# Gated MLP of a two-layer decoder trunk: eight of 44 gate tiles as seven block products instead of eight

## Chip, cores and metric

The kernel runs on one core of one Trainium2 chip. The metric is device time in microseconds (us) of one launch; smaller is better. The engines of that core work from separate queues, each strictly in the order in which the program names the instructions: TensorE (PE in the profile), VectorE (DVE), ScalarE (ACT), GpSimd (POOL) and SyncE (SP), whose queue issues nearly all of the DMAs here.

## What is computed

A decoder trunk of two layers over 256 tokens of width 2048. Each layer has an attention mixer (block-sparse attention in layer 0, latent attention in layer 1) and then a gated MLP with an inner width of 5632. Only the MLP's gate product `h @ w_gate` changes here.

```python
def conv_glu_ffn(h, w_gate, w_up, conv_w, conv_b, w_down):
    g = h @ w_gate
    g = causal_depthwise_conv(g, conv_w, width=3) + conv_b     # along the tokens
    return (jax.nn.silu(g) * (h @ w_up)) @ w_down

for i in range(2):
    x = x + mixer_i(rms_norm(x, attn_norm[i]))
    x = x + conv_glu_ffn(rms_norm(x, ffn_norm[i]), ...)
```

All of it is float32.

## The kernel before

**Three products for one.** Every float32 operand of a large product is split into a high and a low part: the high part is a cast to the type float32r, the low part is the operand minus the high part. A product then takes three matmuls: high by high, high by low, low by high. The normed input `h` of the MLP lies in SBUF as such parts, with features on the partitions: 16 tiles of 128 features, each with 256 high and 256 low token columns. The norm's gain is in `h`; its factor per token (`rstd_b`, spread over the partitions) is multiplied in after the gate and the up product.

**Pieces.** Weights stream from HBM in units of 128 x 1024 words, each of two pieces of 128 x 512. A piece of the MLP's gate or up weight holds four 128 x 128 blocks: four feature tiles of the input (`kq` counts these fours, 0 to 3) by one tile of 128 inner features. `Stream.split` (lines 113 to 130) makes the two parts of a piece: ACT casts (`whi`, line 125), DVE subtracts (`wlo`, line 126). There are five buffers for each part, so that the parts of piece p take the place of those of p - 5.

**The order of the work** is written out by hand. `quanta` lists the steps, one piece each. At step q the main loop (the end of `trunk`) first splits all pieces up to q + 3, then issues the matmuls of piece q, and then whatever `at(q, ...)` has put beside it:

```python
ws.split(q + min(1 + q // 6, AHEAD_PIECES))     # AHEAD_PIECES = 4: pieces below q + 4
f(*args, *ws.take(q))
for g, gargs in (..., *side.pop(q, [])):
    g(*gargs)
```

**The MLP.** `plan_gate_up` goes through 44 tiles of 128 inner features. For each it adds four gate pieces and four up pieces. A piece is 12 matmuls (`feat_major`, lines 301 to 303): for each of its four blocks high weight by high `h`, high weight by low `h`, low weight by high `h`. The weight block is the stationary operand, and the 256 tokens move. Beside the matmuls, by step after a tile's last gate piece q:

- q: `evac_gate` (DVE, line 970), PSUM times `rstd_b` into `g`
- q + 1: `conv_last` (ACT, line 977); q + 2: `conv_rest` (two DVE instructions, line 983); q + 3: `silu` (ACT, line 988)
- q + 4, which is the last up piece: `scaled` and `product` (DVE, lines 991 and 994); then `high` (ACT, line 997) and `low` (DVE, line 1001) make the parts of the inner activation `a`, one of 44 tiles in SBUF.

The down product (`plan_down_feat`) reads `a` after all 44 tiles are there. At the start of a gate and up stage, q0, lie remains of the norm: PE sums at step q0 + 2 (line 370), PE transposes at q0 + 3 (line 380), and then ACT's copy of `rstd_b` (line 384), for which the first `evac_gate` waits. The attention stages have helpers that the change uses too: `cross_out` and `cross_in` turn a matrix by 32 x 32 transposes on DVE (line 410) and a way through HBM (four DMAs out, one back).

Of the kernel before, what the change touches and what calls it, by code (L numbers as in the profile page):

```python
# [54 lines left out]
H_TILES = 0, 4, 16  # L55


class Halves:


    def __init__(self, tiles):
        self.tiles = tiles
# [4 lines left out]
        return self.tiles[i][p, k - H_TILES[i], s]  # L67


class Stream:  # L70

    def __init__(self, nc, raw_pool, part_pool, units, starts):
# [3 lines left out]
        self.pieces = [(u, i, n) for u, (_, k, n) in enumerate(units) for i in range(k)]  # L78
        self.raw, self.parts = {}, {}
        self.loaded = self.split_to = 0  # L80

    def load(self, upto):
# [30 lines left out]
    def split(self, upto):  # L113
        while self.split_to < min(upto, len(self.pieces)):
            i = self.split_to
            u, j, n = self.pieces[i]
            self.load(u + AHEAD_UNITS)
            w = self.raw[u][:, j * n : (j + 1) * n]
            b, c = self.starts(u, j)
            hi = self.part_pool.tile([P, 512 + ROOM], F32R, name="whi")[:, b : b + max(n, 512)]  # L120
            lo = self.part_pool.tile([P, 512 + ROOM], F32R, name="wlo")[:, c : c + max(n, 512)]
            if i == 0:
                self.nc.vector.tensor_copy(hi[:, :n], w)
            else:
                self.nc.scalar.copy(hi[:, :n], w)  # L125
            self.nc.vector.tensor_tensor(  # L126
                lo[:, :n], w, hi[:, :n].bitcast(F32), op=ALU.subtract
            )
# [8 lines left out]
def trunk(ctx: ExitStack, tc: tile.TileContext, a, out):  # L137
# [30 lines left out]
    units += units_of("ffn_gu0")  # L168
    units += units_of("ffn_down0")
    units += units_of("mla_wq_a")  # L170
    units += units_of("mla_wqr")
    units += units_of("mla_wkv_a", 2 * KVN)
# [2 lines left out]
        for name in names:  # L175
            units += grouped(name, 1, g)
    units += units_of("mla_wo")
    units += units_of("ffn_gu1")
    units += units_of("ffn_down1")
    def starts(u, j):  # L180

        if units[u][2] > 512:
            return 0, 0
        return BY_TOKEN if u < 96 or 400 <= u < 444 else BY_FEATURE

    assert len(units) == 740
    ws = Stream(nc, raw_pool, part_pool, units, starts)


    att = ExitStack()  # L190
# [71 lines left out]
    def add(f, *args):  # L262
        quanta.append((f, args))
        return len(quanta) - 1
# [679 lines left out]

    ffn = {}

    def open_ffn(layer):
        if layer == 0:
            att.close()
        else:  # L950
            att2.close()
        ffn["stack"] = ExitStack()
        ffn["pool"] = ffn["stack"].enter_context(tc.tile_pool(name=f"ffn{layer}", bufs=2))
        ffn["a"] = ffn["pool"].tile([P, NF, 2 * S], F32R, name="a", bufs=1)
        ffn["g"] = [ffn["pool"].tile([P, S + 2], F32, name=f"g{i}", bufs=1) for i in range(2)]
        for g in ffn["g"]:
            nc.vector.memset(g[:, 0:2], 0.0)

    class FTile:
        def __init__(self, layer, j, norm):  # L960
            self.layer, self.j, self.norm = layer, j, norm
            self.gate, self.up = {}, {}

        def cw(self, i):
            c = C_CW + (self.layer * 3 + i) * NF + self.j
            return par[:, c : c + 1]

        def evac_gate(self):
            self.g = ffn["g"][self.j % 2]
            nc.vector.tensor_tensor(  # L970
                self.g[:, 2:], self.gate["acc"][:, :S], self.norm.rstd_b, op=ALU.mult
            )
# [26 lines left out]
        def low(self):  # L999
# [2 lines left out]
                a_[:, self.j, S:], self.c, a_[:, self.j, :S].bitcast(F32), op=ALU.subtract  # L1002
            )

    def plan_gate_up(layer, norm):
        for j in range(NF):
            f = FTile(layer, j, norm)
            for kind, st in (("g", f.gate), ("u", f.up)):
                for kq in range(4):
                    q = add(lambda t_hi, t_lo, n, st=st, kq=kq: feat_major(  # L1010
                        st, lambda: norm.h, 4 * kq, KD - 1, kq == 0, t_hi, t_lo, n))
                if kind == "g":
                    if j == 0:
                        at(q, open_ffn, layer)
                    at(q, f.evac_gate)
                    at(q + 1, f.conv_last)
                    at(q + 2, f.conv_rest)
                    at(q + 3, f.silu)
                    at(q + 4, f.scaled)
                else:  # L1020
                    at(q, f.product)
                    at(q + 1, f.high)
                    at(q + 2, f.low)

    plan_gate_up(0, n2)

# [362 lines left out]
    ffn["stack"].close()  # L1389


def wo_order(opened):
# [106 lines left out]
```

## Time and profile before

| | |
|---|---|
| median of three runs | 2069.29 us (2069.16 to 2069.46) |
| span of the profiled execution, first to last instruction | 2067.4 us; what lies outside it is 1.9 us by the median (the page has no other time for that execution) |
| busy: PE, DVE, ACT | 2060.5, 1424.4, 1157.9 us |
| matmuls | 16588 |
| granted TensorE clock | 1.000 |
| moved by DMA | 410.92 MB, mean 199 GB/s |
| first and last gate evacuation | 382.3 us in layer 0, 1819.3 us in layer 1 |

Busy is the time in which an engine had at least one instruction in flight. Matmuls overlap, so the pace of PE is read from the distance of their starts, not from the duration of one. In rows of a timeline the first number is the start, the second the duration; in square brackets stands how long the engine had been idle before and what it waited for.

### The profile page before, as it was taken

What the parts mean: (1) busy time and instruction counts of PE and PEld (TensorE: products, weight loads), DVE (VectorE), ACT (ScalarE), POOL (GpSimd) and SP (SyncE); (2) the same over time, 40 slices, a digit from 0 to 9 for tenths busy, and PEclk for the clock granted to TensorE, in tenths of its full rate; (3) what the DMA queues carried; (4) which work ended last, traced back from release to release, by engine and by line L of the source; (5) the groups of instructions that cost most, each with busy time, mean ns of one, the idle gap of its engine ahead of it and who ended that gap; (6) DMA issues with size and microseconds to landing.
All of it is one profiled execution on the core that took longest, in us unless ns stands there. A gap on an engine that the chain in (4) does not pass through costs nothing.

```text
span 2067.4 us, 42691 instructions
## 1 busy us (share of the span) xinstructions
PE 2060.5 (100%) x16588; PEld 1994.8 (96%) x16588; DVE 1424.4 (69%) x2780; ACT 1157.9 (56%) x2238; POOL 51.1 (2%) x38
## 2 busy tenths in 40 slices
PE   9999999999999999999999999999999999999999
PEld 7888899999999999999999889999999999999999
DVE  7877777766676667655556998767666766665554
ACT  6656666555555555555555786655555555554443
POOL 0000000000000000000000110000000000000000
PEclk9999999999999999999999999999999999999999
DMA  7777776555555565555555646555555565566663
GB/s 276 232 245 224 232 235 209 192 193 195 194 194 194 194 194 195 197 194 193 196 194 158 215 145 189 195 190 191 195 196 195 192 194 195 195 201 202 196 210 125
DMA packets 128251, 410.92 MB, mean 199 GB/s; under 512 B 15008, under 2 KB 28832, under 8 KB 128048
## 3 DMA queue, kind: packets, MB, share of 16 engines
q1 hardware_dynamic: 127728, 407.84, 60.3%
q8 instruction: 129, 2.11, 0.4%
q14 instruction: 74, 0.61, 0.1%
q10 hardware_dynamic: 288, 0.33, 0.1%
q0 software_dynamic: 32, 0.04, 0.0%
HBM read 396.48 MB, written 11.67 MB: 197 GB/s over the span
## 4 chain that ended last, share of the span: by engine, by line
PE 96%; DVE 2%; DMA 1%; ACT 0%; issue 0%; POOL 0%; SPq 0%; DVEq 0%; ACTq 0%; POOLq 0%
PE acc L301 26%; PE acc L303 26%; PE acc L302 26%; PE acc L275 14%; DVE wlo L126 1%; PE sc L551 0%; PE sc L549 0%; PE sc L550 0%; DMA raw<-in_mla_wqn 0%; PE sc L652 0%; PE sc L571 0%; PE tp L542 0%; DVE ss L454 0%; DMA xT<-in_xT 0%; ACT sq L450 0%
## 5 line engine op out<-in xcount | busy, mean ns | idle before, releaser
L126 DVE TENSOR_TENSOR wlo<-raw,whi 128x512 fp32r<-128x512 f32 x1464 | 998.7, 689 | 370.6 <-ACT whi L125 366.5
L125 ACT CAST whi<-raw 128x512 fp32r<-128x512 f32 x1463 | 870.1, 618 | 458.6 <-PE acc L302 215.3
L301 PE MATMUL acc<-h,whi 128*128 128x256 f32 x2880 | 796.1, 276 | 0.0
L303 PE MATMUL acc<-h,wlo 128*128 128x256 f32 x2880 | 795.8, 276 | 0.0
L302 PE MATMUL acc<-h,whi 128*128 128x256 f32 x2880 | 795.7, 276 | 0.0
L301 PEld LDWEIGHTS acc<-h,whi 128*128 128x128 f32 x2880 | 540.8, 188 | 0.0
L302 PEld LDWEIGHTS acc<-h,whi 128*128 128x128 f32 x2880 | 540.8, 188 | 0.0
L303 PEld LDWEIGHTS acc<-h,wlo 128*128 128x128 f32 x2880 | 540.8, 188 | 0.0
L302 PE MATMUL acc<-a,whi 128*128 128x256 f32 x1408 | 389.0, 276 | 0.0
L301 PE MATMUL acc<-a,whi 128*128 128x256 f32 x1408 | 389.0, 276 | 0.0
L303 PE MATMUL acc<-a,wlo 128*128 128x256 f32 x1408 | 389.0, 276 | 0.0
L275 PE MATMUL acc<-whi,h 128*128 128x512 f32 (+1 forms) x896 | 266.1, 378 | 0.7 <-ACT h L323 0.7
L301 PEld LDWEIGHTS acc<-a,whi 128*128 128x128 f32 x1408 | 264.4, 188 | 0.0
L302 PEld LDWEIGHTS acc<-a,whi 128*128 128x128 f32 x1408 | 264.4, 188 | 0.0
L303 PEld LDWEIGHTS acc<-a,wlo 128*128 128x128 f32 x1408 | 264.4, 188 | 0.0
L275 PEld LDWEIGHTS acc<-whi,h 128*128 128x128 f32 x896 | 164.9, 188 | 31.1 <-ACT h L323 1.2
L275 PE MATMUL acc<-wlo,h 128*128 128x512 f32 (+1 forms) x448 | 168.7, 377 | 0.2 <-DVE wlo L126 0.2
L301 PE MATMUL acc<-oT,whi 128*128 128x256 f32 x512 | 142.7, 279 | 0.0
L303 PE MATMUL acc<-oT,wlo 128*128 128x256 f32 x512 | 141.7, 277 | 0.0
L302 PE MATMUL acc<-oT,whi 128*128 128x256 f32 x512 | 141.6, 277 | 0.0
L970 DVE TENSOR_TENSOR g<-acc,rstd_b 128x256 f32<-128x256 f32 x88 | 37.5, 426 | 126.8 <-PE acc L303 123.9
L977 ACT ACTIVATE c<-g,par 128x256 f32<-128x256 f32 x88 | 53.1, 603 | 107.8 <-DVE g L970 107.8
(197 smaller groups left out, 1616.2 us busy)
## 6 DMA issues: line engine op xcount, KB each, us to landing
raw<-in_ffn_gu SPq DMA_DIRECT2D x352, 512.0 KB, 4.4
raw<-in_ffn_down SPq DMA_DIRECT2D x176, 512.0 KB, 4.7
raw<-in_moba_wk SPq DMA_DIRECT2D x32, 512.0 KB, 5.7
raw<-in_moba_wv SPq DMA_DIRECT2D x32, 512.0 KB, 5.3
raw<-in_moba_wo SPq DMA_DIRECT2D x32, 512.0 KB, 4.5
raw<-in_mla_wo SPq DMA_DIRECT2D x32, 512.0 KB, 4.0
raw<-in_moba_wq SPq DMA_DIRECT2D x24, 512.0 KB, 6.2
there<-blk SPq DMA_DIRECT2D x36, 128.0 KB, 2.5
```

Of the source, the lines that this page charges most:

```text
L125: self.nc.scalar.copy(hi[:, :n], w)
L126: self.nc.vector.tensor_tensor(lo[:, :n], w, hi[:, :n].bitcast(F32), op=ALU.subtract)
L275: mm(state["acc"][t][:, :n], src[:, kt, c : c + P], (t_lo if part == 1 else t_hi)[:, :n], start=kt == 0 and part == 0, stop=kt == k_last a ...
L301: mm(o, w_hi, src[:, kt, :S], start=first and k == 0, stop=False, skip_group_check=True)
L302: mm(o, w_hi, src[:, kt, S:], start=False, stop=False, skip_group_check=True)
L303: mm(o, w_lo, src[:, kt, :S], start=False, stop=kt == k_last, skip_group_check=True)
L970: nc.vector.tensor_tensor(self.g[:, 2:], self.gate["acc"][:, :S], self.norm.rstd_b, op=ALU.mult)
L977: nc.scalar.activation(self.c, self.g[:, 2:], AF.Identity, bias=par[:, cb : cb + 1], scale=self.cw(2))
```

## The change

In each layer eight of the 44 gate tiles, in two groups of four (tiles 15 to 18 and 19 to 22), are no longer four pieces each. The product of a group is taken for each `kq` as a two by two block product, tokens (two halves of 128) by inner features (two pairs of tiles) by features (even and odd tiles), in the scheme that needs seven products of sums of blocks in place of eight products of blocks (15 additions). For each of the four `kq` of a group there are seven block pieces of six matmuls, so 168 matmuls for a group where four tiles took 192. Here a token block is the stationary operand, and 256 weight columns move. The sums over the four `kq` lie in four PSUM banks for the length of a group.

Four sums of token blocks are made at the start of each stage, in four rounds three steps apart (`tokens`: four ACT instructions; `token_sums`: two DVE instructions in each of two steps; `token_high`: ACT; `token_low`: DVE). The weights of a group's gate tiles come by loads of their own, four of 256 KB for each `kq`; four sums of weight blocks for each `kq` are DVE instructions. After a group the seven sums are mixed (`mixed`, five DVE instructions in three steps) and turned to features on the partitions (`cross`: two DVE transposes and four DMAs, `crossed`: one DMA). `evac_gate` of a block tile reads that in place of PSUM, just ahead of the tile's up pieces.

The order: 24 plain pieces; 28 times one block piece and two plain ones; four plain pieces; again 28 times; then what is left. Plain pieces keep their form; the tile of `a` is cut in four, and the parts that are filled last hold the raw weights, the token sums and the mixed sums until then.

The diff, cut (the class `Inner`, the unit lists and the offsets of the layer-1 weights are left out; by the latter some pieces of the latent attention and of its output product lie at other offsets in their buffers):

```diff
+BLOCK_LEAD, BLOCK_GAP, BLOCK_EVERY = 24, 4, 2
+BLOCK_GROUPS = tuple(range(15, 19)), tuple(range(19, 23))
...
 class Stream:
...
             u, j, n = self.pieces[i]
-            self.load(u + AHEAD_UNITS)
-            w = self.raw[u][:, j * n : (j + 1) * n]
-            b, c = self.starts(u, j)
+            if u is None:
+                b, c = BY_FEATURE
+                w = j()
+            else:
+                self.load(u + AHEAD_UNITS)
+                w = self.raw[u][:, j * n : (j + 1) * n]
+                b, c = self.starts(u, j)
...
+            for f, args in self.after.pop(i, ()):
+                f(*args)
...
+    class Blocks:
...
+        def tokens(self, kq):
+            y = self.rawq[0].rearrange("p (k s) -> p k s", k=4)
+            for k in range(4):
+                j = 4 * kq + k
+                g = par[:, self.norm.gain_col + j : self.norm.gain_col + j + 1]
+                nc.scalar.activation(y[:, k], xT[:, j, :], AF.Copy, scale=g)
...
+        def token_sums(self, step):
+            a11, a12, a21, a22, s = self.quarters()
+            for out, x, y, op in (
+                ((s[:, 0], a21, a22, ALU.subtract), (s[:, 2], a11, a21, ALU.subtract)),
+                ((s[:, 1], s[:, 0], a11, ALU.subtract), (s[:, 3], s[:, 1], a12, ALU.add)),
+            )[step]:
+                nc.vector.tensor_tensor(out, x, y, op=op)
+
+        def token_high(self, kq):
+            nc.scalar.copy(self.parts[:, :, 2 * kq : 2 * kq + 2, 0], self.quarters()[-1])
+
+        def token_low(self, kq):
+            hi, lo = (self.parts[:, :, 2 * kq : 2 * kq + 2, h] for h in range(2))
+            nc.vector.tensor_tensor(lo, self.quarters()[-1], hi.bitcast(F32), op=ALU.subtract)
...
+        def weight_sum(self, i):
+            b11, b21, b12, b22 = (self.quarter(half, e) for half in range(2) for e in range(2))
+            t1, t3, t2 = (self.total(k) for k in range(3))
+            out, x, y = ((t1, b11, b12), (t3, b12, b22), (t2, t1, b22), (t1, t2, b21))[i]
+            nc.vector.tensor_tensor(out, x, y, op=ALU.add)
...
+        def products(self, g, kq, s, t_hi, t_lo, n):
...
+            for i in range(2):
+                p = 2 * kq + i
...
+                w_hi, w_lo = t_hi[:, i * S : (i + 1) * S], t_lo[:, i * S : (i + 1) * S]
+                mm(o, x[:, 0], w_hi, start=opens and i == 0, stop=False, skip_group_check=True)
+                mm(o, x[:, 1], w_hi, start=False, stop=False, skip_group_check=True)
+                mm(o, x[:, 0], w_lo, start=False, stop=last and i == 1, skip_group_check=True)
...
+            if step == 0:
+                nc.vector.tensor_copy(z[:, 0:2], two(0))
+                nc.vector.tensor_tensor(z[:, 0:2], z[:, 0:2], twice(1), op=ALU.add)
+            elif step == 1:
+                nc.vector.tensor_tensor(z[:, 3], z[:, 1], self.bank[1][:, S:], op=ALU.add)
+                nc.vector.tensor_tensor(z[:, 2:6:3], twice(3), z[:, 1:4:2], op=ALU.subtract)
+            else:
+                nc.vector.tensor_tensor(z[:, 1:5:3], z[:, 2:4], two(2), op=ALU.add)
...
     def plan_gate_up(layer, norm):
...
+                if (kq, s) == (3, 6):
+                    for i in range(3):
+                        at(q + 1 + i, block.mixed, i)
+                    at(q + 5, block.cross)
+                    at(q + 7, block.crossed)
...
+            if kq == 0 and up and f.block is not None:
+                plan_gate(f, q - 1)
+            if kq == 3:
+                (plan_up if up else plan_gate)(f, q)
+
+        for kq in range(4):
+            q = q0 + 4 + 3 * kq
+            at(q, block.tokens, kq)
+            at(q + 1, block.token_sums, 0)
+            at(q + 2, block.token_sums, 1)
+            at(q + 2, block.token_high, kq)
+            at(q + 3, block.token_low, kq)
+        for half in range(2):
+            at(q0 + 17, block.load, 0, 0, half)
+        quads = [(g, kq) for g in range(len(BLOCK_GROUPS)) for kq in range(4)]
+        for n, (g, kq) in enumerate(quads):
+            p = [block_pieces[layer, g, kq, s] for s in range(7)]
+            for i, k in enumerate((p[0] + 1, p[1], p[1] + 2, p[3] + 1)):
+                ws.after.setdefault(k, []).append((block.weight_sum, (i,)))
+            if n + 1 < len(quads):
+                ws.after.setdefault(p[2] + 2, []).append((block.load, (*quads[n + 1], 1)))
+                ws.after.setdefault(p[3] + 1, []).append((block.load, (*quads[n + 1], 0)))
```

More of the change, by code (lines that the diff above doesn't have):

```diff
@@ L55 @@
 H_TILES = 0, 4, 16
+BLOCK_LEAD, BLOCK_GAP, BLOCK_EVERY = 24, 4, 2
+BLOCK_GROUPS = tuple(range(15, 19)), tuple(range(19, 23))
+A_TILES = 0, 19, 23, 39, NF
 class Halves:
@@ L67, in __getitem__, with __init__, words @@
         return self.tiles[i][p, k - H_TILES[i], s]
+class Inner:
+    def __init__(self, pool):
+        self.pool, self.tiles = pool, {}
+    def words(self, i, dt):
+        n = (A_TILES[i + 1] - A_TILES[i]) * 2 * S
+        return self.pool.tile([P, n], dt, name=f"a{i}", bufs=1)
+    def __getitem__(self, at):
+        p, j, s = at
+        i = max(i for i in range(4) if A_TILES[i] <= j)
+        if i not in self.tiles:
+            self.tiles[i] = self.words(i, F32R).rearrange("p (j s) -> p j s", s=2 * S)
+        return self.tiles[i][p, j - A_TILES[i], s]
 class Stream:
-    def __init__(self, nc, raw_pool, part_pool, units, starts):
+    def __init__(self, nc, raw_pool, part_pool, units, starts, pieces):
         self.starts = starts
@@ L77, in __init__ @@
         self.units = units
-        self.pieces = [(u, i, n) for u, (_, k, n) in enumerate(units) for i in range(k)]
-        self.raw, self.parts = {}, {}
+        self.pieces = pieces
+        self.raw, self.parts, self.after = {}, {}, {}
         self.loaded = self.split_to = 0
@@ L177, in trunk @@
     units += units_of("mla_wo")
-    units += units_of("ffn_gu1")
+    fixed = gate_up_units(1)
     units += units_of("ffn_down1")
@@ L952, in open_ffn @@
         ffn["stack"] = ExitStack()
+        ffn["turn"] = 0
         ffn["pool"] = ffn["stack"].enter_context(tc.tile_pool(name=f"ffn{layer}", bufs=2))
-        ffn["a"] = ffn["pool"].tile([P, NF, 2 * S], F32R, name="a", bufs=1)
+        ffn["a"] = Inner(ffn["pool"])
+        ffn["a"][:, 0, :]
+        blocks[layer].open()
         ffn["g"] = [ffn["pool"].tile([P, S + 2], F32, name=f"g{i}", bufs=1) for i in range(2)]
@@ L962, in __init__ @@
             self.gate, self.up = {}, {}
+            self.block = None
         def cw(self, i):
@@ L968, in evac_gate @@
         def evac_gate(self):
-            self.g = ffn["g"][self.j % 2]
+            self.g = ffn["g"][ffn["turn"] % 2]
+            ffn["turn"] += 1
+            if self.block is not None:
+                out, r = (
+                    x.rearrange("p (t i c) -> p t i c", t=NT, i=4) for x in (self.g[:, 2:], self.norm.rstd_b)
+                )
+                nc.vector.tensor_tensor(out, blocks[self.layer].gate(self.block), r, op=ALU.mult)
+                return
             nc.vector.tensor_tensor(
@@ L1003, in low, with plan_gate @@
             )
-    def plan_gate_up(layer, norm):
[L1006 to L1023, printed above, removed]
+    def plan_gate(f, q):
+        at(q, f.evac_gate)
+        at(q + 1, f.conv_last)
+        at(q + 2, f.conv_rest)
+        at(q + 3, f.silu)
+        at(q + 4, f.scaled)
@@ L1389, in trunk, with gate_up_order, full, up @@
     ffn["stack"].close()
+def gate_up_order():
+    def full(j):
+        return [("plain", j, up, kq) for up in range(2) for kq in range(4)]
+    def up(j):
+        return [("plain", j, 1, kq) for kq in range(4)]
+    def group(g):
+        return [("block", g, kq, s) for kq in range(4) for s in range(7)]
+    first_, second = BLOCK_GROUPS
+    plain = []
+    for js, fulls in ((), range(10)), (first_, range(10, 15)), (second, range(second[-1] + 1, NF)):
+        fulls = list(fulls)
+        for j in fulls[:2] if js else fulls:
+            plain += full(j)
+        for i, j in enumerate(js):
+            plain += up(j)
+            if i + 2 < len(fulls):
+                plain += full(fulls[i + 2])
+        for j in fulls[2 + len(js) :] if js else ():
+            plain += full(j)
+    order = plain[:BLOCK_LEAD]
+    plain = plain[BLOCK_LEAD:]
+    for g in range(len(BLOCK_GROUPS)):
+        for one in group(g):
+            order += [one, *plain[:BLOCK_EVERY]]
+            plain = plain[BLOCK_EVERY:]
+        order += plain[:BLOCK_GAP]
+        plain = plain[BLOCK_GAP:]
+    return order + plain
 def wo_order(opened):
```

126 lines of the change are left out of this document (117 added, 9 removed).

## Prediction

> **What bounds the kernel now.** I read the page first: engine shares and the chain that ended last.
>
> ```profile
> span 2067.4 us, 42691 instructions
> PE 2060.5 (100%) x16588; PEld 1994.8 (96%) x16588; DVE 1424.4 (69%) x2780; ACT 1157.9 (56%) x2238; POOL 51.1 (2%) x38
> PE 96%; DVE 2%; DMA 1%; ACT 0%; issue 0%; POOL 0%; SPq 0%; DVEq 0%; ACTq 0%; POOLq 0%
> L126 DVE TENSOR_TENSOR wlo<-raw,whi 128x512 fp32r<-128x512 f32 x1464 | 998.7, 689 | 370.6 <-ACT whi L125 366.5
> L125 ACT CAST whi<-raw 128x512 fp32r<-128x512 f32 x1463 | 870.1, 618 | 458.6 <-PE acc L302 215.3
> ```
>
> 96% of the chain is PE. ACT waits 215 us for PE to give part buffers back: the splitting runs ahead of PE and is held by it. So matmuls taken away are time won, as long as the split parts keep coming. Whether they do is a matter of one tile of the gate and up stage, so next its DVE timeline, then the stretches:
>
> ```profile
> 403.71 0.43 DVE L970 TENSOR_TENSOR g<-acc,rstd_b 128x256 f32<-128x256 f32 x1 [1.44 <-PE acc L303]
> 404.06 0.68 DVE L126 TENSOR_TENSOR wlo<-raw,whi 128x512 fp32r<-128x512 f32 x1
> 405.32 0.69 DVE L126 TENSOR_TENSOR wlo<-raw,whi 128x512 fp32r<-128x512 f32 x1 [0.59 <-ACT whi L125]
> 405.93 1.00 DVE L983 SCALAR_TENSOR_TENSOR c<-g,par,c 128x256 f32<-128x256 f32 x2
> 406.85 0.69 DVE L126 TENSOR_TENSOR wlo<-raw,whi 128x512 fp32r<-128x512 f32 x1
> 407.93 0.69 DVE L126 TENSOR_TENSOR wlo<-raw,whi 128x512 fp32r<-128x512 f32 x1 [0.40 <-ACT whi L125]
> 408.54 0.42 DVE L991 TENSOR_TENSOR c<-c,rstd_b 128x256 f32<-128x256 f32 x1
> 409.15 0.42 DVE L994 TENSOR_TENSOR c<-c,acc 128x256 f32<-128x256 f32 x1 [0.20 <-PE acc L303]
> 409.49 0.68 DVE L126 TENSOR_TENSOR wlo<-raw,whi 128x512 fp32r<-128x512 f32 x1
> 410.57 0.69 DVE L126 TENSOR_TENSOR wlo<-raw,whi 128x512 fp32r<-128x512 f32 x1 [0.39 <-ACT whi L125]
> 411.18 0.42 DVE L1001 TENSOR_TENSOR a<-c,a 128x256 fp32r<-128x256 f32 x1
> ...
> 414.59 0.43 DVE L970 TENSOR_TENSOR g<-acc,rstd_b 128x256 f32<-128x256 f32 x1 [1.44 <-PE acc L303]
> ```
>
> ```profile
> core 0: us, PE busy (x) PEld busy (x) DVE busy (x) ACT busy (x) POOL busy (x), PEclk, DMA share, GB/s
> 408.66:419.54 10.88, 10.88 (x99) 10.88 (x98) 7.57 (x15) 5.79 (x11) 0.00 (x0) 1.00 0.60 194
> ```
>
> A tile lasts 414.59 - 403.71 = 10.88 us: eight pieces of 1.36 us, 96 matmuls 113.3 ns apart. DVE instructions overlap a little, so what one costs is the distance of starts: 0.61 us for a `wlo` (405.32 to 405.93), 0.34 for 256 columns (409.15 to 409.49), 0.92 for the two of L983. A tile's own DVE work is thus 0.35 + 0.92 + 3 x 0.34 = 2.29 us beside eight `wlo`. DVE looks a third free, but part of that can't be used: its waits for `whi` (0.59, 0.40, 0.39: 1.4 us a tile) come about because ACT, in order, does `conv_last`, `silu` or `high` ahead of the next `whi`. True reserve is a lead: after a gate evacuation the next `wlo` ends 1.0 us later, and PE wants it 4.3 us later (three pieces, and the third matmul of the fourth): 3.2 us.
>
> **What PE is relieved of.** Gone: 8 tiles x 48 matmuls x 2 layers = 768. Added: 4 groups x 168 = 672. Their form is new (tokens stationary, 256 weight columns moving); the nearest row is the attention's, with tokens stationary and 512 columns:
>
> ```profile
> 162.32 10.91 PE acc L275 x48
> ```
>
> 227.3 ns for 512 columns, 113.6 for 256: the same pace. So PE saves 96 x 0.1133 = 10.9 us, 5.4 a layer; a block piece lasts 0.68 us. If offsets or operand roles cost a few per cent of 672 x 0.113 = 76 us, that is up to 2 or 3 us, the other way below nothing unlikely; I take none. The same for the attention pieces at other offsets (some two dozen pieces of 1.36 us: under 1 us).
>
> **What the rounds of token sums cost.** This is the large term. They lie at steps 4 to 16 of each stage (steps counted from q0), where plain pieces run as before. The rows that price them:
>
> ```profile
> 379.69 0.34 PE tp L370 x4
> 381.52 0.36 PE tp L380 x2
> 376.10 0.51 ACT L323 ACTIVATE h<-xT,par 128x256 fp32r<-128x256 f32 x1 [2.67 <-DVE xT L389]
> 376.51 0.40 ACT L342 ACTIVATE nsq<-xT 128x256 f32<-128x256 f32 x1
> 377.53 2.17 ACT L125 CAST whi<-raw 128x512 fp32r<-128x512 f32 x4
> 382.18 0.62 ACT L125 CAST whi<-raw 128x512 fp32r<-128x512 f32 x1
> 382.78 0.60 ACT L977 ACTIVATE c<-g,par 128x256 f32<-128x256 f32 x1
> 384.43 1.28 ACT L988 ACT_TABLE_LOAD x1
> ```
>
> ```profile
> L410 DVE STREAM_TRANSPOSE sblk<-s 128x768 f32<-128x768 f32 x11 | 10.7, 973 | 0.1
> L410 DVE STREAM_TRANSPOSE blk<-qk 128x512 f32<-128x512 f32 x20 | 13.1, 688 | 0.0
> L997 ACT CAST a<-c 128x256 fp32r<-128x256 f32 x88 | 35.9, 408 | 104.7 <-DVE c L994 104.7
> ```
>
> On ACT `tokens` is four gained copies 0.41 us apart, 1.64; a `whi` follows another after 0.52. `token_high` has 1024 columns: from 256 (0.41) to 512 (0.62) a cast grows by 0.21 per 256, so 1.04. On DVE `token_sums` is 2 x 0.34 in each of two steps; `token_low`, 1024 columns at 0.285 more per 256 (688 to 973), lasts about 1.25 and holds DVE 1.15.
>
> By throughput alone, DVE in a round has 3 x 0.61 + 4 x 0.34 + 1.15 + 3/8 x 2.29 = 5.2 us, PE 4.08. But the queues are in order, and the steps hang on each other across engines. One round: ACT does `whi`, then `tokens` (1.64), and only then the next `whi` (0.57); DVE has `wlo` (0.61), the first sums (0.68), `wlo` (0.61), the second sums (0.68); only then can `token_high` run (1.04), behind it the third step's `whi` (0.62), and DVE waits for that. With 0.1 for hand-overs 6.6 us; the tiles' own work on DVE between (0.3 to 0.9 a round) makes it about 7.1, where PE wants 4.08.
>
> I went through the steps with these prices, counting from 381.88, when PE starts piece 4 (the transposes at 381.52 end there; 379.69 is the end of step 2). At step q the piece that is split is q + 3. The first round: at step 4 the `whi` of piece 7 starts at 0.30 and `conv_last` at 0.90, as in the rows; `tokens` holds ACT from 1.41 to 3.05. Step 5: `whi` 8 to 3.67, `wlo` 8 to 4.4, `conv_rest` to 5.3, first sums to 5.9. Step 6: `whi` 9 is ready early, `wlo` 9 ends 6.6, the second sums 7.3; the table load of the first `silu`, hidden today, is hidden in that too; `token_high` runs from 7.35 to 8.4. Step 7: `whi` 10 to 8.9, `wlo` 10 to 9.7; then `scaled`, `product` and `token_low` hold DVE to 11.4, and the next `tokens` holds ACT to 10.5. And so on:
>
> | piece | 9 | 10 | 11 | 12 | 13 | 14 | 15 | 16 | 17 | 18 | 19 | 20 |
> |---|---|---|---|---|---|---|---|---|---|---|---|---|
> | its `wlo` ends | 6.6 | 9.7 | 12.1 | 13.4 | 16.8 | 18.9 | 20.6 | 23.6 | 26.3 | 27.6 | 31.3 | 33.1 |
> | PE wants it | 7.0 | 8.4 | 11.0 | 13.5 | 14.8 | 18.1 | 20.3 | 21.9 | 25.0 | 27.7 | 29.0 | 32.7 |
> | PE stands still | 0 | 1.3 | 1.1 | 0 | 2.0 | 0.8 | 0.3 | 1.7 | 1.3 | 0 | 2.3 | 0.4 |
>
> PE wants a `wlo` at the piece's third matmul, 0.23 after its start, and ends the piece 1.13 after that; each standstill shifts what follows. The sum is 11.1 us. Bounds: throughput alone gives 4 x (5.2 - 4.08) = 4.5 less the lead of 3.2, so 1.3; full durations in place of distances add 0.8 a round, so some 14. I take the count by steps, since it is the only one that knows the order of the queues. Both layers start the stage alike.
>
> **What follows.** The first block loads wait until `token_low` has read their buffer, at 32.5 by that count.
>
> ```profile
> raw<-in_ffn_gu SPq DMA_DIRECT2D x352, 512.0 KB, 4.4
> ```
>
> At 4.4 us they land about 37; the first block's `whi` is wanted at 38.3. It just fits, but the sums of the second half and `conv_rest` of tile 2 then queue up: 0 to 2 us, I take 0.9 (pieces 25 and 28). Raw loads behind them on SP wait some 3 us with six units (over 15 us) in hand: nothing.
>
> First group: 28 x 0.68 + 56 x 1.36 = 95.2 us of PE. DVE has 84 `wlo` and 16 weight sums at 0.61, seven tiles at 2.29, and at most 1.4 x 7 of waits for `whi`: 86.8. Nothing lost. Second group: also 95.2 on PE; DVE 61.0 for the hundred of 512 columns, 9.5 tiles at 2.29 (the block tiles have all their own work within four up pieces), and for `mixed` and the transposes of the first group 6 x 0.61 + 0.34 = 4.0 (a PSUM operand costs nothing more: 0.43 in L970 beside 0.42 in L991): 86.8, with at most 9.5 x 1.4 of waits 100. Weight sums fill some of these. Over PE by 0 to 4.8 less the lead of 3.2: 0 to 1.6 a layer, I take 0.5. `crossed` holds SP about as long as such steps did in attention (128 KB landing in 2.5 us), with more units in hand; its data are wanted over ten pieces later: nothing. DMA bytes don't change.
>
> Sum for a layer: -5.4 + 11.1 + 0.9 + 0.5 = +7.1. For both +14: 2067.4 + 14.2 = 2081.6 in the span, and with the 1.9 us outside it 2083.5; I say 2083.
>
> **A rule weighed.** In the DVE rows a 0.43 us instruction is followed after 0.35, and 0.69 after 0.61, and I count by these. The Trainium skill ("VectorE: DVE Perf Modes", The DRAIN you can't avoid) says that an instruction starts only when the pipe has emptied behind the one before, and excepts those that are not held. By the rule without its exception DVE would cost full durations, which is the third rival below. The trace agrees with the exception.
>
> **Rivals.** *Throughput decides, and the change wins.* Should ACT and DVE slip past each other so that only DVE's 5.2 us per round counts, a layer loses 1.3 to 4.5 us against 5.4: 2069.3 - 10.9 + 2.6 to 9 = 2061 to 2067. For it: lead and idle time are there, ACT's share is 56%. Against: every hand-over above is between neighbours in strict queues. The break-even is 5.4 us of standstill a layer. 20%.
>
> *DVE is the bound in the groups.* At full durations a tile's own work is 0.43 + 1.00 + 3 x 0.42 = 2.69, and the second group has 100 x 0.69 + 9.5 x 2.69 + 4.6 = 99 us of DVE without any wait, 4 over PE, and each round grows by 0.8: 7 more a layer, 2098. If only the waits in the groups are worse than I take them, 3 or 4 a layer: 2090. Against it are the distances of starts. 10%.
>
> *The scheme doesn't save.* Six block matmuls at 130 ns instead of 113 would eat the 10.9 us: with the standstill 2094. Against it the L275 row. 4%.
>
> **Numbers.** The forecast has 66%, with a range of its own from 2073 to 2092 (standstill 7 to 14 us in a layer). About 0.2%, 4 us, is what a measurement of this kernel can tell from no change: 2065.2 to 2073.4. Faster: most of the first rival, 14%. Same: the rest of it and the low end of mine, 13%. Slower: 73%. The range of 2064 to 2094 leaves out part of the first rival and the ends of the others.
>
> **What would show it.** Right: 16492 matmuls; the first gate evacuation where it was; between some 390 and 415 us, and again 970 us on, PE idle behind `wlo`, with DVE waiting for `whi` and ACT's `token_high` ahead of that; three steps of a round 7 us apart; then PE full in both groups with matmuls 113 ns apart. Wrong: PE full in those stretches (the first rival); PE idle behind `wlo` in the second group by more than 2 us (the second); block matmuls farther apart (the third).

## The result, and the profile after

The kernel with the change takes 2093.73 us (median; 2093.45 to 2093.89), the one before 2069.24 in the same rounds. The ratio is 1.0118, with a 95% interval from 1.0103 to 1.0132: slower by 24.5 us, in the direction that was forecast (2083). It is beyond the 2073 to 2092 that the forecast gave itself, and only 0.3 us inside the wider range of 2064 to 2094, which takes in most of the rivals. The span grew by 24.2 us, where the sum had 14.2.

The page of the kernel after, with the same lines as were read before:

```profile
span 2091.6 us, 42985 instructions
PE 2069.7 (99%) x16492; PEld 1996.1 (95%) x16492; DVE 1519.0 (73%) x2960; ACT 1201.6 (57%) x2326; POOL 47.2 (2%) x38
PE 93%; DVE 4%; ACT 1%; issue 1%; DMA 1%; DVEq 0%; ACTq 0%
L157 DVE TENSOR_TENSOR wlo<-raw,whi 128x512 fp32r<-128x512 f32 x1400 | 950.4, 689 | 347.5 <-ACT whi L156 341.5
L156 ACT CAST whi<-raw 128x512 fp32r<-128x512 f32 x1399 | 831.4, 618 | 399.5 <-DVE wlo L157 195.6
```

The 96 matmuls are gone (16588 to 16492), and yet PE is busy 9 us longer, since a matmul that is slow, or still in flight when the parts for the next one are late, counts as busy. The second reading is in the last column: the longest wait of ACT's casts was for PE (215.3 us); now it is for DVE's `wlo` (195.6). That wait has hardly grown (192.6 before); it is the wait for PE that fell, to 170.6. PE holds the splitting back less often.

Where the 24.2 us lie is seen at the PE transposes that open and close the stages. First the kernel before, then the one after, both from the chain of waits:

```profile
1098.64 0.34 PE tp L370 x4
1349.22 0.34 PE tp L370 x4
1351.06 0.35 PE tp L380 x2
```

```profile
381.39 0.35 PE tp L437 x2
1109.75 0.34 PE tp L427 x4
1361.70 0.34 PE tp L427 x4
1363.54 0.35 PE tp L437 x2
```

With the starts at 381.52 and 381.39 and the ends of the spans, the MLP of layer 0 takes 717.1 before and 728.4 after (+11.2), attention 250.6 and 252.0 (+1.4), and the MLP of layer 1 716.3 and 728.1 (+11.7). A layer was forecast at +7.1.

Next the rounds themselves. DVE's timeline after, in layer 1, where PE starts piece 4 at 1363.89 (these are the `wlo` of pieces 9, 10, 13, 16 and 19, with the first round's sums between):

```profile
1369.06 0.76 DVE L1042 TENSOR_TENSOR a<-a 128x256 f32<-128x256 f32 x2
1369.73 0.69 DVE L157 TENSOR_TENSOR wlo<-raw,whi 128x512 fp32r<-128x512 f32 x1
1370.33 0.88 DVE L1042 TENSOR_TENSOR a<-a 128x256 f32<-128x256 f32 x2
1372.84 0.69 DVE L157 TENSOR_TENSOR wlo<-raw,whi 128x512 fp32r<-128x512 f32 x1 [1.63 <-ACT whi L156]
...
1380.17 0.69 DVE L157 TENSOR_TENSOR wlo<-raw,whi 128x512 fp32r<-128x512 f32 x1 [1.63 <-ACT whi L156]
...
1387.02 0.69 DVE L157 TENSOR_TENSOR wlo<-raw,whi 128x512 fp32r<-128x512 f32 x1 [1.63 <-ACT whi L156]
...
1394.92 0.69 DVE L157 TENSOR_TENSOR wlo<-raw,whi 128x512 fp32r<-128x512 f32 x1 [1.63 <-ACT whi L156]
```

ACT's timeline beside it:

```profile
1365.30 1.69 ACT L1029 ACTIVATE a<-xT,par 128x256 f32<-128x256 f32 x4
...
1371.24 1.05 ACT L1045 CAST a<-a 128x1024 fp32r<-128x1024 f32 x1 [1.48 <-DVE a L1042]
1372.20 0.61 ACT L156 CAST whi<-raw 128x512 fp32r<-128x512 f32 x1
```

It is the chain of hand-overs that the prediction walked through: `tokens` hold ACT to 1366.99, the second sums end at 1371.21, ACT idles 1.48 us for them, `token_high` runs, only then the next `whi`, and DVE idles 1.63 us for that. The `wlo` of pieces 10, 13, 16 and 19 end 9.6, 17.0, 23.8 and 31.7 us after PE's start of piece 4; the prediction had 9.7, 16.8, 23.6 and 31.3.

### The profile page after: what moved, and what is told of

It is laid out like the page before. It is cut to its first block, busy times and chain, and to the rows that moved or that the text cites. A ratio compares the mean times of both kernels' runs of the same rounds, so it can differ in the third digit from the quotient of the medians.

```text
span 2091.6 us, 42985 instructions
## 1 busy us (share of the span) xinstructions
PE 2069.7 (99%) x16492; PEld 1996.1 (95%) x16492; DVE 1519.0 (73%) x2960; ACT 1201.6 (57%) x2326; POOL 47.2 (2%) x38
## 4 chain that ended last, share of the span: by engine, by line
PE 93%; DVE 4%; ACT 1%; issue 1%; DMA 1%; DVEq 0%; ACTq 0%
PE acc L360 24%; PE acc L359 24%; PE acc L358 24%; PE acc L332 16%; DVE wlo L157 1%; PE tp L1099 1%; PE tp L1097 1%; PE tp L1098 1%; DMA raw<-in_ffn_gu 1%; DVE a L1042 1%; PE sc L1099 1%; PE sc L1097 1%; PE sc L1098 1%; ACT whi L156 0%; PE sc L608 0%
## 5 line engine op out<-in xcount | busy, mean ns | idle before, releaser
L157 DVE TENSOR_TENSOR wlo<-raw,whi 128x512 fp32r<-128x512 f32 x1400 | 950.4, 689 | 347.5 <-ACT whi L156 341.5
L156 ACT CAST whi<-raw 128x512 fp32r<-128x512 f32 x1399 | 831.4, 618 | 399.5 <-DVE wlo L157 195.6
L358 PE MATMUL acc<-h,whi 128*128 128x256 f32 x2624 | 727.9, 277 | 9.3 <-ACT whi L156 9.3
L360 PE MATMUL acc<-h,wlo 128*128 128x256 f32 x2624 | 729.3, 278 | 6.3 <-DVE wlo L157 6.0
L359 PE MATMUL acc<-h,whi 128*128 128x256 f32 x2624 | 726.7, 277 | 0.0
L358 PEld LDWEIGHTS acc<-h,whi 128*128 128x128 f32 x2624 | 493.3, 188 | 11.8 <-ACT whi L156 11.7
L360 PEld LDWEIGHTS acc<-h,wlo 128*128 128x128 f32 x2624 | 493.7, 188 | 10.7 <-DVE wlo L157 10.3
L359 PEld LDWEIGHTS acc<-h,whi 128*128 128x128 f32 x2624 | 493.4, 188 | 0.0
L332 PEld LDWEIGHTS acc<-wlo,h 128*128 128x128 f32 x448 | 84.2, 188 | 16.2 <-DVE wlo L157 1.6
```

Of the source, the lines that this page charges most:

```text
L156: self.nc.scalar.copy(hi_, w)
L157: self.nc.vector.tensor_tensor(lo_, w, hi_.bitcast(F32), op=ALU.subtract)
L332: mm(state["acc"][t][:, :n], src[:, kt, c : c + P], (t_lo if part == 1 else t_hi)[:, :n], start=kt == 0 and part == 0, stop=kt == k_last a ...
L358: mm(o, w_hi, src[:, kt, :S], start=first and k == 0, stop=False, skip_group_check=True)
L359: mm(o, w_hi, src[:, kt, S:], start=False, stop=False, skip_group_check=True)
L360: mm(o, w_lo, src[:, kt, :S], start=False, stop=kt == k_last, skip_group_check=True)
```

## The experiments

Times of the parts, from the same transposes, in us (the kernels are told below):

| kernel | MLP of layer 0 | attention | MLP of layer 1 |
|---|---|---|---|
| before | 717.1 | 250.6 | 716.3 |
| after | 728.4 | 252.0 | 728.1 |
| rounds alone | 728.9 | 250.6 | 729.3 |
| no low part of the sums | 727.1 | 251.5 | 726.2 |
| no rounds | 715.0 | 252.0 | 714.2 |
| rounds spread | 718.0 | 251.6 | 717.3 |
| rounds spread wider | 716.4 | 251.0 | 715.5 |
| no rounds, roles exchanged | 712.5 | 251.5 | 711.4 |

The theory after the result: the rounds stall PE by hand-overs between queues that work in order (A), and the block pieces cost PE more than their 113 ns a matmul. The rivals: it is the amount of DVE's work that counts; or the lower pace comes from start offsets in SBUF.

### Offsets

```diff
-                b, c = BY_FEATURE
+                b, c = BY_TOKEN
...
-    tok_units = len(units) + 16
+    tok_units = len(units) + 8
```

> The changed kernel with other starts of the split weights inside their buffers: those of the latent attention's pieces as before the change, and block pieces at the start that pieces with moving weights have elsewhere (8 and 8 words in place of 24 and 56). Theory A (the start of an operand sets the pace of matmuls): the latent attention with its output product gets its 1.4 us back, and a block piece with two plain ones goes from 3.453 to 3.40 us, 2.9 us a layer; 2093.7 - 1.4 - 5.8 = 2086.5. Rival B (the loss in the groups comes from the switch between two forms of piece, not from addresses): 2092.3, with 3.453 us as before.

Measured: 2093.23 us beside 2069.61, ratio 1.0114 (1.0099 to 1.0129). Attention falls from 252.0 to 251.2, so 0.8 of its 1.4 us come from the offsets: the change counts eight units too many and so shifts the pieces of the second attention. In three windows of 10 us early in its output product 86 or 87 matmuls are issued in place of 88 to 90 (in unbroken stretches 120.0 ns apart, not 113.8); with the old offsets 88 to 90 again. In the groups the sum did not change: a block piece and its two plain ones still take 3.45 us. Which matmuls are slow did change: with the starts 24 and 56 the six of the block piece and six behind it (some 118 ns each), with 8 and 8 the six and only three behind (some 119). Offsets explain most of the attention's loss; of the block pieces' loss the two pairs of starts that were tried explain nothing.

### No low part of the sums

```diff
-                    x = self.parts[:, {2: 3, 3: 0, 4: 2, 5: 1}[s], p]
+                    x = self.parts[:, {2: 3, 3: 0, 4: 2, 5: 1}[s], p, 0:1].to_broadcast([P, 2, P])
...
-            at(q + 3, block.token_low, kq)
```

> The changed kernel without token_low: the low parts of the token sums are left out, and the block products that use sums take the high part twice. This takes 1.15 us of DVE from each round and nothing from ACT. Theory A (a round is a chain of hand-overs between ACT and DVE in the order of their queues, with token_low beside the ACT copies, not on the chain): a round goes from 7.1 to about 6.8 us, PE stands still 10 us a layer in place of 11.5 to 12.8, about 2090. Rival B (DVE's throughput sets a round): DVE has 4.05 us a round, PE 4.08, so hardly any standstill; about 2070.

Measured: 2090.24, ratio 1.0101 (1.0084 to 1.0118). The layers get 1.3 and 1.8 us shorter. `token_low` holds DVE for 1.15 us, 4.6 in the four rounds; if DVE's amount of work set the pace, up to that would have come back. Most of it lay in DVE's waits for ACT. That speaks for A and against throughput.

### The rounds alone

```diff
-    tok_units = len(units) + 16
+    tok_units = len(units) + 8
...
-    for g in range(len(BLOCK_GROUPS)):
-        for one in group(g):
-            order += [one, *plain[:BLOCK_EVERY]]
...
+    return [one for j in range(NF) for one in full(j)]
```

The weight sums and the block loads are taken out with the groups.

> All 44 gate tiles as plain pieces, as before the change, but with the four rounds of token sums at their steps; the sums are not used. Theory A (the rounds by themselves stop PE): 2069.2 + 11.5 + 12.8 = 2093, or 2091 by the count of the prediction. Rival B (the standstill needs the block loads or the groups behind): 2069 to 2075.

Measured: 2094.83, ratio 1.0121 (1.0106 to 1.0136). All 16588 matmuls of before, and the rounds of sums cost 11.8 us in layer 0 and 13.0 in layer 1. That is as much as the whole change.

### No rounds

```diff
-                    x = self.parts[:, {2: 3, 3: 0, 4: 2, 5: 1}[s], p]
+                    t = s % 2
+                    x = self.norm.h[:, 2 * p + 1, :].rearrange("p (h t s) -> p h t s", h=2, t=NT)[:, :, t]
...
-            at(q, block.tokens, kq)
-            at(q + 1, block.token_sums, 0)
-            at(q + 2, block.token_sums, 1)
-            at(q + 2, block.token_high, kq)
-            at(q + 3, block.token_low, kq)
```

> The changed kernel without the rounds: the token sums are left out, and the products that use them take plain token blocks. Theory A: 2093.7 less 24.3 for the rounds and about 3 for the first block loads, which then have no work in front of them: 2066 to 2067, with the 3.453 us in the groups unchanged and PE otherwise full. Rival B (DVE is also the bound in the groups): 2075 or more, with PE idle behind the parts in the second group.

Measured: 2066.64, ratio 0.9985 (0.9976 to 0.9994). The rest of the change gains, but 2.1 us a layer, not the 5.4 that 48 matmuls are worth. PE's first block piece in layer 0, in the kernel without rounds and in the one after:

```profile
408.82 0.28 PE L1098 MATMUL tp<-whi,h 128*128 128x256 f32 x1
```

```profile
420.63 0.28 PE L1097 MATMUL tp<-whi,h 128*128 128x256 f32 x1
```

The stage starts at 381.39 in the first and the last, so the rounds hold PE up by 420.63 - 408.82 = 11.8 us.

### Rounds spread

```diff
-            q = q0 + 4 + 3 * kq
-            at(q, block.tokens, kq)
-            at(q + 1, block.token_sums, 0)
-            at(q + 2, block.token_sums, 1)
-            at(q + 2, block.token_high, kq)
-            at(q + 3, block.token_low, kq)
+            q = q0 + (4, 18, 34, 52)[kq]
+            at(q, block.tokens, kq, 0)
+            at(q + 2, block.tokens, kq, 1)
+            at(q + 4, block.token_sums, 0)
+            at(q + 5, block.token_sums, 1)
+            at(q + 7, block.token_high, kq)
+            at(q + 9, block.token_low, kq)
...
-            at(q0 + 17, block.load, 0, 0, half)
+            at(q0 + 6, block.load, 0, 0, half)
```

The sums are made in the buffer of the mixed sums, so that the block loads need not wait for them; the offsets of the attention are as before. Nothing is left out.

> The changed kernel with the rounds of token sums spread: they use the place of the mixed sums as scratch, start 4, 18, 34 and 52 steps into the stage, and their parts lie steps apart (two copies, two copies two steps on, sums two and three steps on, high part, low part); the first block loads, no longer behind them, are issued at step 6; starts of the latent attention's pieces as before the change. Nothing is left out. Theory A (the rounds cost what their order and place make of them, and the groups have room on DVE): the 24.3 us of standstill and 3 of the first loads go, as in the run without rounds (2066.6), and 1.4 in the attention: 2065 to 2067, a little faster than before. Rival B (DVE's total is the limit in the stage): four rounds are 10 us of DVE a layer that the groups have to find, so PE waits there for 3 to 6 us a layer: 2072 to 2078.

Measured: 2071.93 beside 2069.89, ratio 1.0009 (1.0000 to 1.0018). Against the kernel without rounds the same work in other places costs 3 us a layer; in the kernel with the change it is 13.4 and 13.9, first block loads included. What is left lies at single triples (a block piece and the two plain ones behind it), where a round falls beside weight sums: 4.04, 3.88 and 4.73 us in place of 3.45.

### Rounds spread wider

```diff
+            q = q0 + (4, 12, 38, 60)[kq]
+            steps = (0, 2, 4, 5, 7, 9) if kq < 2 else (0, 3, 7, 10, 14, 18)
+            for n, (f, *args) in zip(steps, (
+                (block.tokens, kq, 0), (block.tokens, kq, 1), (block.token_sums, 0),
+                (block.token_sums, 1), (block.token_high, kq), (block.token_low, kq),
+            )):
+                at(q + n, f, *args)
```

> As the spread version, with two rounds ahead of the first group (starts at 4 and 12 steps) and two later and wider in it (38 and 60 steps, parts 3 or 4 steps apart). Nothing is left out. Theory A (what is left of the rounds' cost is bunching: a round close to the first weight sums of a four, where the lead of 3.2 us is short): from 3 us a layer to 1 or less, 2067 to 2069. Rival B (DVE's total is what is missing): no change, 2071 to 2072.

Measured: 2068.61 beside 2069.64, ratio 0.9996 (0.9987 to 1.0005): no difference that can be measured from before, and 25 us less than the kernel with the change. Its page, and the stretch from the start of the stage to its second block piece, with two of the four rounds in it:

```profile
PE 2059.4 (100%) x16492; PEld 1991.6 (96%) x16492; DVE 1517.2 (73%) x2960; ACT 1198.6 (58%) x2326; POOL 47.5 (2%) x38
```

```profile
core 0: us, PE busy (x) PEld busy (x) DVE busy (x) ACT busy (x) POOL busy (x), PEclk, DMA share, GB/s
381.20:412.76 31.56, 31.42 (x272) 31.07 (x273) 25.80 (x50) 22.22 (x43) 0.00 (x0) 1.00 0.62 207
```

DVE and ACT have as many instructions as after (2960 and 2326) and nearly the same busy time, and PE has work for 31.42 of 31.56 us. The first block piece starts at 408.88, 0.25 us later from the stage's start than without rounds. The amount of work was not the trouble; its coming all at once was. A layer here is 1.3 to 1.4 us longer than without rounds.

### Rounds on GpSimd

```diff
-                nc.scalar.activation(y[:, k], xT[:, j, :], AF.Copy, scale=g)
+                nc.gpsimd.tensor_scalar(y[:, k], xT[:, j, :], g, None, op0=ALU.mult)
...
-                nc.vector.tensor_tensor(out, x, y, op=op)
+                nc.gpsimd.tensor_tensor(out, x, y, op=op)
...
-            nc.vector.tensor_tensor(lo, self.quarters()[-1], hi.bitcast(F32), op=ALU.subtract)
+            nc.gpsimd.tensor_tensor(lo, self.quarters()[-1], hi.bitcast(F32), op=ALU.subtract)
```

The rounds begin at steps 4, 24, 46 and 67, with the high and the low part 17 steps later.

> As the spread version, but the gained copies, the token sums and the low parts run on GpSimd, idle in this stage; only the high parts stay on ACT, 17 steps behind the sums. Nothing is left out. Theory A (a round costs what it puts into the queues of ACT and DVE): the 3 us a layer that the spread rounds still cost go, 2065 to 2067 as without rounds. Rival B (GpSimd's reads slow the DVE instructions beside them, or GpSimd takes over a microsecond for 256 columns and ACT then waits): at the 3 us of the spread version or worse, 2071 and more.

Measured: 2079.01 beside 2069.64, ratio 1.0046 (1.0033 to 1.0058), 7 us more than with the rounds spread on ACT and DVE. GpSimd's rows, and DVE's at the same time:

```profile
381.27 4.02 POOL L1030 TENSOR_SCALAR a<-xT,par 128x256 f32<-128x256 f32 x4
385.38 4.03 POOL L1043 TENSOR_TENSOR a<-a 128x256 f32<-128x256 f32 x4
406.21 2.40 POOL L1050 TENSOR_TENSOR a<-a,a 128x1024 fp32r<-128x1024 f32 x1 [16.80 <-ACT a L1046]
```

```profile
385.56 2.37 DVE L157 TENSOR_TENSOR wlo<-raw,whi 128x512 fp32r<-128x512 f32 x2
405.82 3.07 DVE L1179 SCALAR_TENSOR_TENSOR c<-g,par,c 128x256 f32<-128x256 f32 x2
```

Two `wlo` take 2.37 us instead of 1.29, and `conv_rest`, 1.00 us where GpSimd is idle, takes 3.07 and ends 0.28 us behind GpSimd's instruction. DVE is not relieved by this but held up. The Trainium skill ("SBUF — State Buffer", Who interferes with whom) says that a DVE instruction with two SBUF inputs contends with a GpSimd instruction that reads SBUF; these rows agree. How much it costs depends on GpSimd's instruction: beside TENSOR_SCALAR, which reads one matrix, the `wlo` at 383.81 kept its 0.69 us, and the most that such a `wlo` took was 0.88.

### What slows the block pieces: pairs, roles, length, sums

Without rounds, 30 matmuls of a triple should take 30 x 0.1133 = 3.40 us; they take 3.453. There are 56 triples a layer, so 3.0 us. First, two block pieces in a row and four plain ones, without rounds:

```diff
-        for one in group(g):
-            order += [one, *plain[:BLOCK_EVERY]]
-            plain = plain[BLOCK_EVERY:]
+        for n, one in enumerate(group(g)):
+            order.append(one)
+            if n % 2:
+                order += plain[: 2 * BLOCK_EVERY]
+                plain = plain[2 * BLOCK_EVERY :]
```

> As the run without rounds (token sums left out, plain token blocks in their place), but block pieces come in pairs: two block pieces and four plain ones in place of one and two. Theory A (0.053 us are lost at each change between the two forms of piece): half as many changes, 14 x 0.053 = 0.75 us a group, 3.0 in all: 2063.7, and 6.85 us for a pair with its four plain pieces. Rival B (each block piece costs its own 0.053 us, or a matmul of that form is slower): 2066.6 as without pairs, 6.91 us.

Measured: 2068.26, ratio 0.9989 (0.9980 to 0.9998). Six pieces take 6.88 us: 0.080 too many for two block pieces, between the two theories. Pairs come too fast for DVE early in a group (7.77 and 7.66 us for the first pair of each, 7.36 for the fifth of the second), which eats the gain. The same order with the rounds spread:

> Rounds spread as above and block pieces in pairs; nothing is left out. If each change between forms costs 0.053 us: 3.0 us under the spread version, 2062 to 2064. If each block piece costs it: as the spread version, 2065 to 2067. If pairs of short pieces outrun DVE (two parts' work of 1.2 us and a weight sum within 1.36 us of PE, against a lead of 3.2 us): over 2067.

Measured: 2072.39, ratio 1.0012 (1.0003 to 1.0021); in the first group the first pair takes 8.26 us, the fourth 8.34 and the seventh 7.16. No help.

Then three kernels without rounds, timed once each, in which the distances of starts in the trace are what counts. The roles of the operands:

```diff
-                mm(o, x[:, 0], w_hi, start=opens and i == 0, stop=False, skip_group_check=True)
-                mm(o, x[:, 1], w_hi, start=False, stop=False, skip_group_check=True)
-                mm(o, x[:, 0], w_lo, start=False, stop=last and i == 1, skip_group_check=True)
+                y = self.norm.h[:, 2 * p + int(s > 0), :]
+                mm(o, w_hi[:, :P], y[:, :S], start=opens and i == 0, stop=False, skip_group_check=True)
+                mm(o, w_hi[:, P:], y[:, S:], start=False, stop=False, skip_group_check=True)
+                mm(o, w_lo[:, :P], y[:, :S], start=False, stop=last and i == 1, skip_group_check=True)
```

> What costs the 0.053 us by which a block piece and two plain pieces (24 + 6 matmuls) take longer than 30 x 0.1133 = 3.40 us? The kernel is the one without rounds of token sums (sums left out, plain token blocks in the products; 3.45 us in every triple there), and here the operands of the block pieces change places as well: the weight block is stationary (128 columns of it) and 256 token columns move, as in plain pieces; so it computes something else, with as many matmuls of the same size. If the change of roles between plain and block pieces is what slows the matmuls behind it to 116 to 120 ns: triples of 3.40, and the two MLP layers some 3 us shorter each than in the kernel without rounds. If the roles have no part in it: 3.45 again. I hold the change of roles for a little likelier than not.

Twice as many matmuls in a block piece:

```diff
-                mm(o, x[:, 1], w_hi, start=False, stop=False, skip_group_check=True)
...
+                for rep in range(2):
+                    mm(o, x[:, 0], w_hi, start=opens and i == 0 and rep == 0, stop=False, skip_group_check=True)
+                    mm(o, x[:, 1], w_hi, start=False, stop=False, skip_group_check=True)
+                    mm(o, x[:, 0], w_lo, start=False, stop=last and i == 1 and rep == 1, skip_group_check=True)
```

> The kernel without rounds again (token sums left out), but each block piece issues each of its six matmuls twice, so that it is as long as a plain piece: 12 matmuls, 36 in a triple, 4.08 us at 113.3 ns. If the 0.053 us come with a piece that is short (its parts have to be waited for and handed back twice as often in that time), triples take 4.08. If they come with a change of the kind of piece, whatever its length: 4.13. If each slow matmul belongs to the block piece itself (its operands): above 4.13, up to 4.19.

And no weight sums after the first:

```diff
-            for i, k in enumerate((p[0] + 1, p[1], p[1] + 2, p[3] + 1)):
+            for i, k in enumerate((p[0] + 1, p[1], p[1] + 2, p[3] + 1) if n == 0 else ()):
```

> The kernel without rounds again (token sums left out), and of the sums of weight blocks only those of the first kq of the first group are made, and used for all others: 4 x 7 x 2 = 56 DVE instructions fewer, whose strided reads and writes lie beside the block pieces. If these writes to the buffers beside PE's reads slow the matmuls: triples of less than 3.45, down to 3.40, from the second kq on. If DVE has no part in it: 3.45 throughout, and the same layer times as in the kernel without rounds.

Measured: 2060.71, 2144.58 and 2066.60 us, beside 2070.42 for the kernel before. Starts on PE's timeline, first without rounds (a block piece, the plain piece behind it, the next block piece), then with roles exchanged, then with twelve matmuls:

```profile
433.02 0.28 PE L1098 MATMUL tp<-whi,h 128*128 128x256 f32 x1
...
433.73 0.28 PE L358 MATMUL acc<-h,whi 128*128 128x256 f32 x1
...
434.44 0.28 PE L358 MATMUL acc<-h,whi 128*128 128x256 f32 x1
...
436.48 0.28 PE L1098 MATMUL tp<-whi,h 128*128 128x256 f32 x1
```

```profile
432.52 0.28 PE L1099 MATMUL tp<-h,whi 128*128 128x256 f32 x1
...
435.92 0.28 PE L1099 MATMUL tp<-h,whi 128*128 128x256 f32 x1
```

```profile
441.89 0.28 PE L1099 MATMUL tp<-whi,h 128*128 128x256 f32 x1
...
443.30 0.28 PE L358 MATMUL acc<-h,whi 128*128 128x256 f32 x1
...
446.05 0.28 PE L1099 MATMUL sc<-whi,h 128*128 128x256 f32 x1
```

In the first, the six matmuls of the block piece take 0.71 us, the six behind it another 0.71 (118 ns each), and the remaining 18 2.04 (113 ns). With the roles of plain pieces the triple is 3.40 to the hundredth, and both layers are 2.5 and 2.8 us shorter: the cost comes with the exchanged roles of the block piece. The twelve block matmuls take 1.41 us, 117.5 ns each, and their triple 4.16 in place of 4.08. So the excess is 0.053 for six and 0.080 for twelve, the same 0.080 as for the pairs, which are twelve in a row as well: worked out from these two, some 0.027 at each change back and 0.0045 for each block matmul. The longer piece thus fell where only a part that grows with the block matmuls puts it, above 4.13: every block matmul is slow, however many come in a row. Without weight sums it stays at 3.45: these sums have no part in it. (What they do cost is the 0.3 us at the start of the second group, which is gone there.)

So it need not be the change between two kinds of piece that slows the block matmuls; the form itself may be slow at this width. A row of the kernel before, in the attention, has tokens stationary too, and 288 weight columns moving, in a long run of its own kind:

```profile
1128.18 0.29 PE L275 MATMUL acc<-wlo,h 128*128 128x288 f32 x1
...
1134.14 0.29 PE L275 MATMUL acc<-wlo,h 128*128 128x288 f32 x1
```

That is 45 matmuls, 132.4 ns apart, where the pace of a plain piece (113.3 for 256 columns) would give 127.5: 5 ns too many each, as in the block pieces, with no change of kind. No run has block matmuls of 256 columns alone, or at other starts than the two pairs above, so these causes are not told apart, and why PE is slowed, and why some plain matmuls behind a block piece are slowed as well, stays open.

## Why the prediction came out as it did

**The rounds, right in kind and nearly in size.** The count by steps gave 11.1 us of standstill a layer; measured at the first block piece it is 11.8 in layer 0, and 12.9 in layer 1 (1403.89 - 1363.54 = 40.35, against 27.43 without rounds). Rounds alone cost 11.8 and 13.0. The first rival, that throughput decides, is refuted twice: PE stands still although DVE is busy for only 26.5 of the stage's first 39 us, and the same work spread wider costs a tenth. The extra microsecond in layer 1 is PE's clock, which no step of the prediction looked at. The windows of after, behind the last round of layer 1:

```profile
core 0: us, PE busy (x) PEld busy (x) DVE busy (x) ACT busy (x) POOL busy (x), PEclk, DMA share, GB/s
1392.96:1395.70 2.74, 0.81 (x6) 0.41 (x4) 1.11 (x3) 2.37 (x5) 0.00 (x0) 0.96 0.11 43
1395.70:1398.82 3.12, 3.12 (x14) 3.12 (x15) 3.12 (x6) 1.58 (x4) 0.00 (x0) 0.50 0.60 186
1398.82:1403.89 5.07, 5.07 (x45) 5.07 (x45) 1.92 (x5) 1.74 (x3) 0.00 (x0) 0.99 0.97 295
```

After 2 us without a matmul (1392.96 to 1394.94) the granted clock is 0.50 for 3.1 us: 14 matmuls, 0.21 us apart instead of 0.113, some 1.4 us, of which the splitting gains a little lead back.

**What PE is relieved of: the mis-sized step.** 96 matmuls less are worth 10.9 us; their number and the kernel with exchanged roles (9.7 us under before, in one run of each) bear that out. But the prediction said of offsets or operand roles "up to 2 or 3 us ... I take none". The roles cost 56 x 0.053 = 3.0 us in each layer, 5.9 in all: more than the bound, and more than half of the saving. The step that failed is the choice of the row: 512 columns at 227.3 ns were halved for 256. The same line of the same profile has 288 columns at 132.4 ns, where the pace of 512 would give 127.9; and matmuls of one kind in a row can't show what happens to the plain ones behind. The third rival (matmuls at 130 ns) had the right suspect, at about twice the size, and its sign, block matmuls farther apart than 113 ns, was there.

**Attention at other offsets.** Forecast under 1 us, measured 1.4, of which the old offsets gave 0.8 back; the other 0.6 is not explained. Kernels with the old offsets lie between 250.6 and 251.6 themselves.

**First block loads.** Forecast 0.9. The issue and the first `whi` that waits for it, in layer 0 after:

```profile
413.89 1.85 SPq L1056 DMA_DIRECT2D a<-in_ffn_gu  x4
```

```profile
419.66 0.62 ACT L156 CAST whi<-a 128x512 fp32r<-128x512 f32 x1 [1.93 <-DMA a<-in_ffn_gu]
```

The issue is 32.1 us after PE's start of piece 4 (forecast 32.5), but the first `whi` can start only 5.8 us after the first of the four issues, not 4.4. PE has no gap ahead of the first block piece; the two triples from there take 4.60 and 3.87 in place of 3.45 each, 1.6 us, and 1.0 in layer 1 (4.01 and 3.87). It goes with the landing of the load: without rounds these two take 3.45 and 3.49, but in the run without weight sums, which has no rounds either and where ACT waits 2.56 us for the first load, 3.96 and 3.87.

**The groups.** The first loses nothing more to DVE, the second about 0.3 at its start (forecast 0.5). That DVE is the bound at full durations, the second rival (which the prediction once calls the third), did not come about: PE has no gap in a triple but at a group's start, and the `wlo` of 0.69 us at 1369.73 above is followed after 0.60. The rule of the Trainium skill ("VectorE: DVE Perf Modes", The DRAIN you can't avoid) without its exception would have asked for the full 0.69.

The sum, as measured: -5.4 + 11.8 + 3.0 + 1.6 + 0.3 = 11.3 in layer 0 (11.2 by the transposes), -5.4 + 12.9 + 3.0 + 1.0 + 0.3 = 11.8 in layer 1 (11.7), and 1.4 in attention. Of the 10 us that the forecast was short of, 5.9 are the roles, 1.4 the attention, 2.5 the standstill with the clock in it, and 0.8 the first loads, less 0.4 for the second group, within 0.2. So the large term was right for the right reason; that the time still fell inside the wider range is in part luck, since nearly all that was missed lay on one side.

## What to carry to other kernels

Price helper work that crosses engines by walking through the queues step by step: a round that hands over three times between ACT and DVE lasted 7 us though neither had more than 5.2 us to do by the prediction's count, and the same round with its steps a few pieces apart cost a tenth. A saving in matmuls is worth its count only at the old pace: look for the row of the new form that is nearest in size (288 columns here, not 512), and where no row has it beside the old form, carry a bound for that into the forecast and not only into the range.

## What the runs showed of the chip

- Matmuls with activations stationary and 256 weight columns moving, among pieces with weights stationary, are some 118 ns apart instead of 113, and so are three to six plain ones behind them (by the start offsets): 0.053 us for a piece of six, 0.080 for twelve. With 288 columns, in a row of their own kind, they are 132.4 ns apart, not 127.5.
- A 2 us standstill was followed by 3.1 us at clock 0.50 in layer 1. All four kernels with bunched rounds have a clock of 0.83 over the 10 us from 1390 (3.4 us at half), and the four with spread rounds 1.00. As long a standstill in layer 0 (410.79 to 412.81) left the clock at 1.00. The Trainium skill ("TensorE: Matmul & The Clock Gate", Part 1: The HAM clock gate) puts the half clock down to an idle window of about 3.4 us that runs freely, and its end to a busy window of that length; the length of the slow stretch agrees, but the pause here was only 2 us.
- By start offsets in SBUF alone, stretches of the attention's output product ran at 120.0 or 113.8 ns a matmul: 86 or 87, or 88 to 90 in 10 us.
- A GpSimd TENSOR_TENSOR of 2.40 us stretched a pair of DVE instructions from 1.00 to 3.07 us.
